# Six fewer transfers in a matmul with bias and residual: merged loads, merged last stores, and the residual added last for 24 tiles

## Chip, cores, metric

The kernel runs on one core of a Trainium2 chip. The metric is the device time of one execution in microseconds (us). The engines have short names: PE multiplies matrices (TensorE; PEld are its weight loads), ACT is ScalarE, DVE is VectorE, POOL is GpSimd, and SP (SyncE) issues the transfers; PSUM is the memory that PE's results land in, SBUF the one that holds the tiles. The granted clock is the share of PE's full clock that the throttle allowed.

## Reference

```python
batch, m, k, n = 16, 512, 1024, 768          # all float32
out = np.matmul(x, weight) + bias + residual # x: 16x512x1024, residual and out: 16x512x768
```

8192 rows are worked in 64 tiles of 128 rows. Eight tiles make a super tile: 128 partitions hold 8 neighbouring rows each, so a whole super tile of x is one transfer of 4 MB (32 KB in one piece per partition), and one of the residual or the output is 3 MB (24 KB per partition).

## The kernel before

x is cast to bf16 on ACT, transposed on PE, copied from PSUM to SBUF on DVE (`xt`), and multiplied on PE. There are two buffers for x, four for residual and output (`ro`, used in place), four for `tmp`. All loads and stores are issued in program order by SP.

```python
X_BUFS = 2; RO_BUFS = 4; TMP_BUFS = 4; EARLY = 12
def load_x(S, j0=0, j1=J):        # rows j0..j1 of super tile S, in one transfer
    ...
    K_(nc.sync.dma_start(out=x_sb[S][:, j0:j1, :], in_=x_d[S, :, j0:j1, :]))
# load_res and store are written the same way

def pool_add(t):                  # POOL: ro += tmp (early tiles), or ro += bias
    r = row(t)
    K_(nc.gpsimd.tensor_add(out=r, in0=r, in1=tmp[t] if t < EARLY else bias_sb))
def finish(t, n0=0, nl=N):        # DVE: empties PSUM
    p = po[t][:, n0:n0 + nl]
    if t < EARLY: tmp[t] = ring(...); nc.vector.tensor_add(out=tmp[t], in0=p, in1=bias_sb)
    else:         nc.vector.tensor_add(out=row(t, n0, nl), in0=p, in1=row(t, n0, nl))
# [...] start-up: x of super tile 0 in five pieces, the weights in four, residual 0 in two
    load_x(1, 0, 4)
    load_res(0, 4, 8)
    load_x(1, 4, 6)
    load_res(1, 0, 4)
    load_x(1, 6, 8)
    load_res(1, 4, 8)
# [...]
    for t in range(HEAD, n_t):
        cast(t + 2)
        S, j = divmod(t, J)
        if (t + 2) % J == J - 1:
            if S == 0:
                for j0 in (0, J // 2):
                    load_x(X_BUFS, j0, j0 + J // 2)
                    load_res(X_BUFS, j0, j0 + J // 2)
            else:
                load_x(S + X_BUFS)
                load_res(S + X_BUFS)
            if 1 <= S < n_s - 1:
                store(S - 1)
        # [...] the tile's 16 matmuls, with the transposes of tile t + 1 among them; finish; pool_add
        if S == n_s - 1 and j == 0:
            store(S - 1)
        if S == n_s - 1 and j == J // 2:
            store(S, 0, J // 2)
        if S == n_s - 1 and j > J // 2:
            store(S, j - 1, j)
    # [...] the last tile, in two column chunks, each finished and stored by itself
```

In the early tiles the sum of PSUM and bias goes to `tmp`, and POOL adds it to the residual when that has landed: DVE can empty PSUM without the residual. In the later tiles POOL adds the bias to the residual beforehand, and DVE needs both.

## Time and profile before

| | before |
|---|---|
| time, median of 6 runs | 211.26 us (211.13 to 211.57) |
| span of the profiled run | 209.4 us |
| PE busy | 200.6 us |
| share of the main DMA queue | 97.8% |
| moved by DMA | 87.2 MB |

The page of the profile, before: the busy line (busy us, share of the span, instructions), two lines of the slices (a digit is the share in a fortieth of the span, 9 for 90% or more), the DMA queues (packets, MB, share of 16 engines), and the chain that ended last.

```profile
...
PE 200.6 (96%) x1274; PEld 130.6 (62%) x1299; DVE 105.0 (50%) x139; ACT 67.6 (32%) x68; POOL 115.4 (55%) x71
...
DMA  6999999999999999999999999999999999999994
...
DMA packets 6208, 87.23 MB, mean 417 GB/s; under 512 B 689, under 2 KB 817, under 8 KB 2098
...
q1 hardware_dynamic: 6192, 87.03, 97.8%
q8 instruction: 10, 0.16, 0.3%
...
PE 95%; issue 1%; DVE 1%
PE po L104 79%; PE pt L95 13%; PE po L172 3%; PE po L192 1%; DVE xt L99 0%; DVE ro L131 0%; DVE warm L158 0%
...
```

PE and DMA are both full from start to end. The chain names PE for 95% of the span. PE ends at 203.2 us, the span is 209.4 us.

The end in stretches of 1 us, before: busy us of each engine with its count of instructions, then granted clock, mean busy share of the 16 DMA engines, GB/s. A share can come out a little over 1, since packets overlap by some ns.

```profile
...
core 0: us, PE busy (x) PEld busy (x) DVE busy (x) ACT busy (x) POOL busy (x), PEclk, DMA share, GB/s
...
201.00:202.00 1.00, 1.00 (x7) 0.42 (x5) 0.68 (x1) 0.00 (x0) 0.00 (x0) 1.00 0.98 409
202.00:203.00 1.00, 1.00 (x10) 0.75 (x8) 0.55 (x1) 0.00 (x0) 0.00 (x0) 1.00 0.99 406
203.00:204.00 1.00, 0.22 (x2) 0.00 (x0) 0.57 (x2) 0.00 (x0) 0.00 (x0) 1.00 0.95 384
204.00:205.00 1.00, 0.00 (x0) 0.00 (x0) 0.00 (x0) 0.00 (x0) 0.00 (x0) 1.00 1.03 404
205.00:206.00 1.00, 0.00 (x0) 0.00 (x0) 0.00 (x0) 0.00 (x0) 0.00 (x0) 1.00 0.73 283
206.00:207.00 1.00, 0.00 (x0) 0.00 (x0) 0.00 (x0) 0.00 (x0) 0.00 (x0) 1.00 0.41 151
207.00:208.00 1.00, 0.00 (x0) 0.00 (x0) 0.00 (x0) 0.00 (x0) 0.00 (x0) 0.76 0.11 39
...
```

PE stops at 203.2, DVE at 203.7. DMA works on at full share to 205 and then fades.

The casts of ACT that wait for x, before (start, us, what, and in brackets the idle time and what ended it). The casts at 51.34 are tiles 16 to 19, the first half of the third x.

```profile
...
36.60 2.00 ACT L87 CAST xb<-x_tile 128x1024 bf16<-128x1024 f32 x2 [2.30 <-DMA x_tile<-in_x_dram]
...
51.34 3.89 ACT L87 CAST xb<-x_tile 128x1024 bf16<-128x1024 f32 x4 [6.60 <-DMA x_tile<-in_x_dram]
59.93 2.00 ACT L87 CAST xb<-x_tile 128x1024 bf16<-128x1024 f32 x2 [4.70 <-DMA x_tile<-in_x_dram]
...
```

PE at the same place, before; the transposes of 128x128 at 55.99 us are tile 16's, one tile (3.04 us) after tile 15's.

```profile
...
52.96 0.60 PE L95 MATMUL pt<-ident,xb 128*128 128x128 f32 x4
...
55.99 0.60 PE L95 MATMUL pt<-ident,xb 128*128 128x128 f32 x4
...
```

### The profile page before, as it was taken

What the parts mean: (1) busy time and instruction counts of PE and PEld (TensorE: products, weight loads), DVE (VectorE), ACT (ScalarE), POOL (GpSimd) and SP (SyncE); (2) the same over time, 40 slices, a digit from 0 to 9 for tenths busy, and PEclk for the clock granted to TensorE, in tenths of its full rate; (3) what the DMA queues carried; (4) which work ended last, traced back from release to release, by engine and by line L of the source; (5) the groups of instructions that cost most, each with busy time, mean ns of one, the idle gap of its engine ahead of it and who ended that gap; (6) DMA issues with size and microseconds to landing.
All of it is one profiled execution on the core that took longest, in us unless ns stands there. A gap on an engine that the chain in (4) does not pass through costs nothing.

```text
span 209.4 us, 3156 instructions
## 1 busy us (share of the span) xinstructions
PE 200.6 (96%) x1274; PEld 130.6 (62%) x1299; DVE 105.0 (50%) x139; ACT 67.6 (32%) x68; POOL 115.4 (55%) x71
## 2 busy tenths in 40 slices
PE   7999999999999999999999999999999999999980
PEld 2556666666666666666666666666666666666640
DVE  0737465455445544554554455445445544555550
ACT  2544315331533062323433053230723133340000
POOL 2000197979999505991099702994069910799000
PEclk9999999999999999999999999999999999999998
DMA  6999999999999999999999999999999999999994
GB/s 237 427 425 427 429 416 428 418 441 419 432 457 440 408 423 426 444 419 435 432 429 435 427 419 446 437 426 423 418 435 437 457 405 416 441 433 430 408 404 155
DMA packets 6208, 87.23 MB, mean 417 GB/s; under 512 B 689, under 2 KB 817, under 8 KB 2098
## 3 DMA queue, kind: packets, MB, share of 16 engines
q1 hardware_dynamic: 6192, 87.03, 97.8%
q8 instruction: 10, 0.16, 0.3%
q14 instruction: 4, 0.03, 0.0%
q10 hardware_dynamic: 2, 0.00, 0.0%
HBM read 61.87 MB, written 25.17 MB: 416 GB/s over the span
## 4 chain that ended last, share of the span: by engine, by line
PE 95%; issue 1%; DVE 1%
PE po L104 79%; PE pt L95 13%; PE po L172 3%; PE po L192 1%; DVE xt L99 0%; DVE ro L131 0%; DVE warm L158 0%
## 5 line engine op out<-in xcount | busy, mean ns | idle before, releaser
L104 PE MATMUL po<-w_sb,xt 128*128 128x512 bf16 (+1 forms) x999 | 175.4, 324 | 1.4
L104 PEld LDWEIGHTS <-xt 128*128 128x128 bf16 x1024 | 100.1, 98 | 59.5 <-DVE xt L99 0.5
L121 POOL TENSOR_TENSOR ro<-ro,bias_sb 128x768 f32<-128x768 f32 x52 | 92.6, 1821 | 51.2 <-DMA ro<-in_residual_dram 41.3
L87 ACT CAST xb<-x_tile 128x1024 bf16<-128x1024 f32 x62 | 62.8, 1045 | 114.6 <-DMA x_tile<-in_x_dram 57.4
L99 DVE COPY xt<-pt 128x512 f32<-128x512 f32 x64 | 44.2, 692 | 86.8 <-PE pt L95 86.6
L131 DVE TENSOR_TENSOR ro<-po,ro 128x768 f32<-128x768 f32 (+2 forms) x53 | 49.4, 934 | 2.9 <-PE po L104 2.8
L95 PE MATMUL pt<-ident,xb 128*128 128x128 f32 x256 | 38.3, 273 | 0.0
L121 POOL TENSOR_TENSOR ro<-ro,tmp 128x768 f32<-128x768 f32 x12 | 21.5, 1817 | 26.2 <-DMA ro<-in_residual_dram 25.0
L95 PEld LDWEIGHTS pt<-ident,xb 128*128 128x128 f32 x256 | 29.8, 141 | 8.3 <-issue 0.8
L129 DVE TENSOR_TENSOR tmp<-po,bias_sb 128x768 f32<-128x768 f32 x12 | 11.4, 949 | 0.5 <-POOL ro L121 0.4
L172 PE MATMUL po<-warm 128*128 128x512 bf16 x15 | 6.0, 574 | 1.2 <-DVE warm L158 1.2
L178 ACT CAST w_sb<-ro 128x768 bf16<-128x768 f32 x4 | 3.3, 832 | 4.1 <-DMA ro<-in_weight_dram 4.1
L172 PEld LDWEIGHTS <-warm 128*128 128x128 bf16 x15 | 1.9, 135 | 4.1 <-issue 2.8
L87 DVE CAST xb<-x_tile 128x1024 bf16<-128x1024 f32 x2 | 1.4, 694 | 5.0 <-DMA x_tile<-in_x_dram 5.0
L180 DVE CAST w_sb<-ro 128x768 bf16<-128x768 f32 x4 | 2.2, 555 | 2.5 <-DMA ro<-in_weight_dram 2.5
L163 ACT ACT_TABLE_LOAD x1 | 1.3, 1283 | 2.0 <-POOL ident masks.py:199 2.0
L192 PE MATMUL po<-tmp 128*128 128x512 f32 (+1 forms) x4 | 1.5, 486 | 0.0
L200 DVE COPY bias_sb<-po 128x768 f32<-128x768 f32 x1 | 1.0, 958 | 0.1
L192 PEld LDWEIGHTS po<-tmp 128*128 128x128 f32 x4 | 0.7, 190 | 0.5 <-issue 0.5
L135 POOL MEMSET tmp<- 128x768 f32 x1 | 0.7, 737 | 0.3 <-POOLq L269 0.3
L158 DVE MEMSET warm<- 128x256 uint32 x1 | 0.3, 272 | 0.9 <-PEq L269 0.9
masks.py:199 POOL TENSOR_SCALAR_AFFINE_SELECT ident<-ident 128x128 f32<-128x128 f32 x1 | 0.3, 292 | 0.1
(8 smaller groups left out, 1.0 us busy)
## 6 DMA issues: line engine op xcount, KB each, us to landing
out_dram<-ro SPq DMA_DIRECT2D x7, 3072.0 KB, 24.2
x_tile<-in_x_dram SPq DMA_DIRECT2D x5, 4096.0 KB, 30.8
ro<-in_residual_dram SPq DMA_DIRECT2D x5, 3072.0 KB, 17.7
ro<-in_residual_dram SPq DMA_DIRECT2D x6, 1536.0 KB, 27.0
x_tile<-in_x_dram SPq DMA_DIRECT2D x3, 2048.0 KB, 25.6
x_tile<-in_x_dram SPq DMA_DIRECT2D x5, 1024.0 KB, 18.3
ro<-in_weight_dram SPq DMA_DIRECT2D x4, 768.0 KB, 9.1
out_dram<-ro SPq DMA_DIRECT2D x1, 1536.0 KB, 11.8
```

The costliest lines, as they stand in the source:

```text
L87: K_(copy(out=xb[t], in_=x_sb[t // J][:, t % J, :]))
L95: K_(nc.tensor.transpose(out=pt[:, c, :], in_=pairs[:, c * P:(c + 1) * P], identity=ident))
L99: K_(nc.vector.tensor_copy(out=xt[t], in_=pt))
L104: K_(nc.tensor.matmul(po[t][:, n0:n0 + nl], lhsT=both[:, e, :], rhs=w_sb[:, c, e, n0:n0 + nl], start=(i == 0), stop=(i == len(steps) - 1),))
L121: K_(nc.gpsimd.tensor_add(out=r, in0=r, in1=tmp[t] if t < EARLY else bias_sb))
L129: K_(nc.vector.tensor_add(out=tmp[t], in0=p, in1=bias_sb))
L131: K_(nc.vector.tensor_add(out=row(t, n0, nl), in0=p, in1=row(t, n0, nl)))
L163: K_(nc.scalar.copy(out=warm_a, in_=warm_a))
L172: K_(nc.tensor.matmul(warm_ps[:, 0:512], lhsT=warm[:, 0:P], rhs=warm, start=True, stop=True))
L178: K_(nc.scalar.copy(out=w_sb[:, c, e, :], in_=w_st[:, c, e, :]))
L180: K_(nc.vector.tensor_copy(out=w_sb[:, c, e, :], in_=w_st[:, c, e, :]))
L192: K_(nc.tensor.matmul(bias_ps[:, n0:n0 + nl], lhsT=ones, rhs=bias_row[:, n0:n0 + nl], start=True, stop=True,))
```

## The change

The intent: fewer and larger transfers, and the residual added last for tiles 12 to 23 too, because the residuals of these tiles now land later.

```diff
-EARLY = 12
+EARLY = 24
@@ start-up
-    load_x(1, 4, 6)
-    load_res(1, 0, 4)
-    load_x(1, 6, 8)
-    load_res(1, 4, 8)
+    load_x(1, 4, 8)
+    load_res(1)
@@ loop
-            if S == 0:
-                for j0 in (0, J // 2):
-                    load_x(X_BUFS, j0, j0 + J // 2)
-                    load_res(X_BUFS, j0, j0 + J // 2)
-            else:
-                load_x(S + X_BUFS)
-                load_res(S + X_BUFS)
+            load_x(S + X_BUFS)
+            load_res(S + X_BUFS)
@@ last stores
-        if S == n_s - 1 and j > J // 2:
-            store(S, j - 1, j)
+        if S == n_s - 1 and j == J - 1:
+            store(S, J // 2, j)
```

## The prediction

> **What bounds the kernel now.** Two things at once. The busy table has PE at 200.6 of 209.4 us, and the chain of waits is 95% PE without a gap above 0.05 us from 21 to 203 us: one tile costs 3.04 us (2.60 of matmuls, 0.44 of transposes). The queue table has the main DMA queue at 97.8%, the slices about 427 GB/s from 5 to 204 us. A super tile (8 tiles) moves 10.5 MB: 24.5 us at 427 GB/s, against 24.3 us of PE work. The Trainium skill ("DMA: Bandwidth & Descriptors", "Anatomy of one DMA") gives about 2 us of fixed cost per DMA; here transfers land 5 to 42 us after their issue because they queue, and the DMA share is about 1.0 in every stretch, so removing five of them frees next to nothing.
>
> **What the change does.**
> - Second x: rows 4-5 land with rows 6-7, about 2.5 us later (estimate: 1.05 MB at 427 GB/s; 36.6 becomes 39). Tile 12 is transposed at 43.85, so PE does not see it.
> - Third x as one 4 MB transfer. Before, its first half landed at 51.34 us (ACT's casts wait for it) and tile 16 was transposed at 55.99, 3.6 us of slack after the 1.05 us cast. The second half landed at 59.93 with 1.57 MB of residual between. Whole, it should land at 59.93 - 1.57/0.427 = 56.25 us. Cast until 57.3: PE should stop about 1.4 us before tile 16. That is on the critical path and PE does not win it back. This is the main cost.
> - Residual added last for tiles 12-23: DVE's add costs 949 against 934 ns, POOL's 1817 against 1821: free. It is needed: the second residual now lands whole near 46.4 us, the third near 63.6; the four tmp buffers let PSUM be emptied anyway (tile 12's add at 51.2 needs POOL's tile 8, done near 48.2). Neither should stop PE.
> - Last stores: rows 4-6 go as one 1.18 MB store when row 6 is finished (201.7 before). Before, row 4 went at about 195.6, DMA stayed busy to about 206, and the last store, issued at 204.0, landed 4.6 us later, behind a backlog. After, the queue runs dry (bytes before these stores end near 202.3), and 1.57 MB, 3.7 us, go out from about 204.7 (with PE 1.4 us late).
>
> **Sum.** +1.4 us PE stall, up to 0.8 us of it absorbed by the backlog at the end, +0.3 us for the emptied queue: about +0.9 us, 212.3 us. Range 211.2 to 213.6. Chances: faster by over 2% 0.01, within 2% 0.95, slower 0.04.
>
> **What would show it.** The chain of waits has a gap of 1 to 2 us near 56 us: PE waits for ACT's cast, the cast for the third x. PE's last matmul ends near 204.6 instead of 203.2; PE busy stays about 200.6. The DMA share falls under 0.8 for 1 to 2 us between 202 and 205. DMA at about 427 GB/s in the middle, no faster.
>
> **What would make it wrong.** Larger packets raising the DMA rate early (the third x lands before 55 us, nothing stalls: about 211.5); the merged load waiting longer at its slowest DMA engine (a stall of 2 to 3 us); tmp buffers holding back DVE, and with it PE, if the second residual lands after 49 us.

## The result

| | before | after |
|---|---|---|
| time, median of 6 runs | 211.26 us | 210.95 us (210.84 to 211.02) |
| ratio, 95% interval | | 0.9983 (0.997 to 0.9996) |
| span of the profiled run | 209.4 us | 209.1 us |
| PE's last matmul ends | 203.2 us | 204.4 us |

A ratio here is the mean time of one kernel's fast runs over the mean of the other's of the same rounds, so not quite the ratio of the medians. The change is worth 0.3 us, 0.17%; predicted were 0.9 us more. A repetition in another set of rounds, with 5 runs, gave 0.9983 again (below).

The page after:

```profile
...
PE 201.1 (96%) x1274; PEld 130.8 (63%) x1299; DVE 105.0 (50%) x139; ACT 68.0 (33%) x68; POOL 115.6 (55%) x71
...
DMA  6999999999999999999999999999999999999966
...
DMA packets 5344, 87.23 MB, mean 417 GB/s; under 512 B 593, under 2 KB 721, under 8 KB 1618
...
q1 hardware_dynamic: 5328, 87.03, 97.8%
...
PE 70%; DMA 25%; issue 1%; ACT 1%; DVE 0%; POOL 0%; ACTq 0%; POOLq 0%
PE po L104 60%; DMA x_tile<-in_x_dram 23%; PE pt L95 10%; DMA tmp<-in_bias_dram 2%; ACT xb L87 1%; DVE ro L131 0%; POOL ident masks.py:197 0%; ACTq L87 0%; POOL tmp L135 0%; POOLq L262 0%
...
```

The casts and PE near the third x, after:

```profile
...
38.95 3.93 ACT L87 CAST xb<-x_tile 128x1024 bf16<-128x1024 f32 x4 [4.70 <-DMA x_tile<-in_x_dram]
56.05 5.93 ACT L87 CAST xb<-x_tile 128x1024 bf16<-128x1024 f32 x6 [13.18 <-DMA x_tile<-in_x_dram]
...
```

```profile
...
53.29 0.60 PE L95 MATMUL pt<-ident,xb 128*128 128x128 f32 x4
...
57.15 0.66 PE L95 MATMUL pt<-ident,xb 128*128 128x128 f32 x4 [0.67 <-ACT xb L87]
...
```

The stop came as predicted. The third x landed whole at 56.05 us (56.25 was said), and tile 16 was transposed at 57.15 instead of 55.99, 1.16 us later. PE's idle time there is shorter, 57.15 - 53.29 - 3.04 = 0.82 us, because PE came to it 0.33 us later than before (tile 15 at 53.29 against 52.96). That difference comes from the start-up and wanders between runs: tile 15's start lies between 52.96 and 53.32 us in the twelve profiles looked at. It does not add to the delay, because x sets the time of tile 16: in the five profiles with the third x whole, ACT's casts of it start at 56.05 to 56.45 us, PE stops for 0.82 to 1.33 us (0.37 of it for DVE in one of them), and tile 16 follows at 57.15 to 57.55; in the others it is at 55.99 to 56.36. From tile 16 to PE's end it is 147.2 us before and 147.3 after. PE ended at 204.4 us, 1.2 us later than before. The chain changed as well: 23% of it is now a wait for x. Yet the kernel became faster. The end in stretches, after (columns as before):

```profile
...
201.00:202.00 1.00, 1.00 (x8) 0.60 (x7) 0.32 (x2) 0.00 (x0) 0.00 (x0) 1.00 0.67 283
202.00:203.00 1.00, 1.00 (x7) 0.43 (x5) 0.90 (x1) 0.00 (x0) 0.00 (x0) 1.00 0.32 135
203.00:204.00 1.00, 1.00 (x9) 0.71 (x8) 0.33 (x1) 0.00 (x0) 0.00 (x0) 1.00 0.41 172
204.00:205.00 1.00, 0.43 (x4) 0.14 (x2) 0.78 (x2) 0.00 (x0) 0.00 (x0) 1.00 1.05 442
205.00:206.00 1.00, 0.00 (x0) 0.00 (x0) 0.00 (x0) 0.00 (x0) 0.00 (x0) 1.00 1.01 406
206.00:207.00 1.00, 0.00 (x0) 0.00 (x0) 0.00 (x0) 0.00 (x0) 0.00 (x0) 1.00 0.85 340
207.00:208.00 1.00, 0.00 (x0) 0.00 (x0) 0.00 (x0) 0.00 (x0) 0.00 (x0) 1.00 0.68 238
...
```

From 201 to 204 us the DMA engines run dry, to a share of 0.32, because rows 4 to 6 are held until row 6 is finished. Then all of them work at full share to 206, and at 207 to 208 still 0.68 of them work, that is 11 engines, where before it was 1.8. Before, a few engines far behind the others ended the kernel; after, all end together.

### The profile page after: what moved, and what is told of

Its sections match the earlier page's. It is cut to its first block, busy times and chain, and to the rows that moved or that the text cites. A ratio compares the mean times of both kernels' runs of the same rounds, so it can differ in the third digit from the quotient of the medians.

```text
span 209.1 us, 3149 instructions
## 1 busy us (share of the span) xinstructions
PE 201.1 (96%) x1274; PEld 130.8 (63%) x1299; DVE 105.0 (50%) x139; ACT 68.0 (33%) x68; POOL 115.6 (55%) x71
## 4 chain that ended last, share of the span: by engine, by line
PE 70%; DMA 25%; issue 1%; ACT 1%; DVE 0%; POOL 0%; ACTq 0%; POOLq 0%
PE po L104 60%; DMA x_tile<-in_x_dram 23%; PE pt L95 10%; DMA tmp<-in_bias_dram 2%; ACT xb L87 1%; DVE ro L131 0%; POOL ident masks.py:197 0%; ACTq L87 0%; POOL tmp L135 0%; POOLq L262 0%
## 5 line engine op out<-in xcount | busy, mean ns | idle before, releaser
L121 POOL TENSOR_TENSOR ro<-ro,bias_sb 128x768 f32<-128x768 f32 x40 | 71.2, 1816 | 34.6 <-DMA ro<-in_residual_dram 24.6
L121 POOL TENSOR_TENSOR ro<-ro,tmp 128x768 f32<-128x768 f32 x24 | 43.1, 1816 | 42.3 <-DMA ro<-in_residual_dram 25.0
L131 DVE TENSOR_TENSOR ro<-po,ro 128x768 f32<-128x768 f32 (+2 forms) x41 | 38.0, 930 | 2.9 <-PE po L104 2.8
L129 DVE TENSOR_TENSOR tmp<-po,bias_sb 128x768 f32<-128x768 f32 x24 | 22.8, 949 | 0.4 <-PE po L104 0.4
```

The source lines that it names most:

```text
L129: K_(nc.vector.tensor_add(out=tmp[t], in0=p, in1=bias_sb))
L131: K_(nc.vector.tensor_add(out=row(t, n0, nl), in0=p, in1=row(t, n0, nl)))
```

## The experiments

**Theory A.** The DMA engine that is furthest behind sets the end of the kernel before. PE has slack, because the last stores queue behind that engine's backlog. The gain comes from the packets of the merged loads.
**Rival B.** The merge of the last stores gained, by fewer completions at the end, and the merged loads cost what PE stops.
**Rival C.** PE's end (or that of the stores) sets the time.

The trace lists every DMA packet with its start, duration and size. The tables below that give time by packet size, or follow one of the 16 engines, were worked out from these records: on one engine, a packet starts 3 or 4 ns before the one ahead of it ends, and every engine has the same sequence of sizes. Where packets of two engines ended at the same moment, the thread could be lost.

### One part alone: only the stores, only the loads

Only the stores:

```diff
 # from the kernel before
-        if S == n_s - 1 and j > J // 2:
-            store(S, j - 1, j)
+        if S == n_s - 1 and j == J - 1:
+            store(S, J // 2, j)
```

> The kernel before, with the last stores merged and nothing else. Theory A (the end is set by the DMA engine that is furthest behind; PE has slack): the merge saves only 0.06 us of packet time (24 packets of 3072 B at 121 ns become 8 of 9216 B at 356 ns on each engine), so the time is within 0.15 us of before. Rival B (the merged store is what gained, by two fewer completions at the end): at least 0.3 us faster than before. My prediction on record would say +0.2 to +0.3 us for an emptied queue.

Measured: 211.34 us against 211.64 for before in the same rounds, ratio 0.9986 (0.9967 to 1.0004). The interval holds both no gain and 0.3 us, so the time alone does not decide between A and B.

Only the loads (and `EARLY = 24`): the kernel after, with the lines above reversed.

> The kernel after, with the last stores row by row as before. PE still stops about 1.2 us near 56 us. Theory A (slowest DMA engine sets the end, larger packets made it faster): 0.2 to 0.4 us faster than before, like the kernel after. Rival B (stores gained, loads cost the PE stop): 0.8 to 1.2 us slower than before.

Measured: 211.53 us, ratio 0.9997 (0.9977 to 1.0017). PE stopped for 0.97 us near 56 us and ended at 204.6 us, and the time was not longer than before's: the 0.8 us that rival B wanted is outside the interval. The 0.2 us that theory A wanted cannot be told from nothing in these rounds (this chip's runs of before spread from 211.32 to 212.54).

What the times could not tell, the bytes can. MB moved by the main queue until 150 us, summed from the packet records of each profiled run:

```
loads as before                  loads merged
before          63.015           after           63.094
stores_only     62.981           loads_only      63.083
before_pe6      62.997           x2_split        63.063
before_pe20     62.979           after_pe6       63.075
                                 after_early12   63.092
                                 after_again     63.087
                                 x2_split_rows   63.079
```

The two groups do not overlap. The means are 62.993 and 63.082 MB; the difference of 0.089 MB is 0.21 us at 427 GB/s. It arises between 30 us (0.003 MB) and 65 us (0.121 MB), where the merged transfers flow, and stays at 0.09 to 0.12 MB. The run with `EARLY = 12` and merged loads is in the right-hand group, so `EARLY` is not the reason. (The failed run with the loads as before stands at 62.962; the run with quarter packets has other packets all through and is left out.) So the merged loads do make DMA faster, by 0.2 us. The packet sizes are the likely reason, since they are what the merge changes there: the median packet of 8 KB took 311 ns (38.9 ns per KB), of 16 KB 614 ns (38.4), of 32 KB 1213 ns (37.9). The sum agrees: all packets of the main queue, less 3.5 ns of overlap each, take 203.50 to 203.76 us per engine in the four runs on the left and 203.31 to 203.41 in the seven on the right. That the gain in time at the end is this 0.2 us is not shown by this run, whose time shows no gain; the last run below (x2_split_rows) is the better test.

### PE without its stop: the third x in two halves

```diff
 # from the kernel after
-            load_x(S + X_BUFS)
+            if S == 0:
+                load_x(X_BUFS, 0, J // 2)
+                load_x(X_BUFS, J // 2, J)
+            else:
+                load_x(S + X_BUFS)
             load_res(S + X_BUFS)
```

> The kernel after, with the third x as two halves one after the other (no residual between), so that PE does not stop near 56 us: the first half should land near 51.3 us, and PE should end near 203.2 us instead of 204.4. Theory A: the time is that of the kernel after, plus at most 0.15 us for packets of 16 KB instead of 32 KB. Rival C (PE's end sets the time): 0.8 to 1.2 us faster than the kernel after, that is 1.1 to 1.5 us faster than before.

ACT, then PE, of this run near tile 16:

```profile
...
51.37 3.89 ACT L87 CAST xb<-x_tile 128x1024 bf16<-128x1024 f32 x4 [8.32 <-DMA x_tile<-in_x_dram]
...
```

```profile
...
53.03 0.60 PE L95 MATMUL pt<-ident,xb 128*128 128x128 f32 x4
...
56.07 0.60 PE L95 MATMUL pt<-ident,xb 128*128 128x128 f32 x4
...
```

The first half landed at 51.4 us, PE went through tile 16 without a stop (56.07 = 53.03 + 3.04) and ended at 203.3 us, as expected. The time: 211.29 us, ratio to before 0.9975 (0.9957 to 0.9993), against 0.9983 for the kernel after. Rival C asked for 1.1 to 1.5 us over before, that is 0.995 or less, which the interval excludes. The end in stretches shows where PE's 1.1 us went:

```profile
...
201.00:202.00 1.00, 1.00 (x6) 0.45 (x5) 0.76 (x1) 0.00 (x0) 0.00 (x0) 1.00 0.66 283
202.00:203.00 1.00, 1.00 (x9) 0.78 (x8) 0.48 (x1) 0.00 (x0) 0.00 (x0) 1.00 0.68 283
...
207.00:208.00 1.00, 0.00 (x0) 0.00 (x0) 0.00 (x0) 0.00 (x0) 0.00 (x0) 0.50 0.10 40
...
```

From 201 to 203 us part of the engines ran dry (0.66, 0.68), because the stores still waited for row 6. At 207 to 208 the share was 0.10 again: 1.6 engines worked on alone, and they ended the kernel whatever PE did. The last packet ended at 208.6 us.

### PE made slower, in both kernels

```diff
 def mms(t, i):
     if i == 0:
         po[t] = psum_o(t)
+        if t == 30:      # n = 6 or 20 matmuls that the tile's own first one overwrites
+            both = xt[t][:, 0, :].bitcast(BF16).rearrange("p (m e) -> p e m", e=2)
+            for _ in range(n):
+                K_(nc.tensor.matmul(po[t][:, 0:512], lhsT=both[:, 0, :],
+                                    rhs=w_sb[:, 0, 0, 0:512], start=True, stop=True))
```

> The kernel before, with six more matmuls of 512 columns (216 ns each, 1.3 us of PE) ahead of tile 30, into PSUM that the tile's own first matmul overwrites; the result is right. Theory A: PE has about 3 us of slack at the end (row 7's stores are issued at 203.2 us and the slowest DMA engine reaches them only near 207), so within 0.15 us of before. Rival C (PE is the bound): 1.3 us slower.

> The kernel after, with the same six matmuls (1.3 us of PE) ahead of tile 30. Theory A: the merged store of rows 4 to 6 began at 203.76 us, just when the slowest DMA engine became free (203.83 us), so no slack is left: 1.0 to 1.3 us slower than the kernel after, 0.7 to 1.1 us slower than before. If the kernel after still had slack, it would stay at 0.3 us faster than before.

> The kernel before, with twenty more matmuls (4.3 us of PE) ahead of tile 30. Theory A: about 3 us of it vanish in the backlog at the end, so 0.9 to 1.8 us slower than before. Rival C (PE is the bound): 4.3 us slower. If DMA alone counted with no limit: same as before.

| added to | PE time added | measured | ratio to before | longer than before |
|---|---|---|---|---|
| before, 6 matmuls | 1.29 us | 211.62 us | 0.9997 (0.998 to 1.0014) | 0.0 us |
| after, 6 matmuls | 1.29 us | 212.49 us | 1.0051 (1.0039 to 1.0064) | 1.1 us (the kernel after: -0.3) |
| before, 20 matmuls | 4.32 us | 212.91 us | 1.0071 (1.0059 to 1.0084) | 1.5 us |

The last column is the difference of the medians of the same rounds; the kernel after was not in these rounds, its -0.3 is from others. Against before, all three are as theory A said (against the kernel after, 1.4 us where 1.0 to 1.3 was said). The kernel before gives away 1.3 us of PE time for nothing. Of 4.3 us it feels 1.5, so its slack on the PE side is about 2.8 us. The kernel after, given the same 1.3 us, loses all of it: its own later PE, and stores that wait for row 6, had used its slack up. The stretches of 2 us of both runs with six matmuls, before first:

```profile
...
201.00:203.00 2.00, 2.00 (x12) 1.08 (x11) 1.32 (x2) 0.00 (x0) 0.00 (x0) 1.00 0.97 404
203.00:205.00 2.00, 1.56 (x12) 0.88 (x9) 1.12 (x3) 0.00 (x0) 0.00 (x0) 1.00 0.85 340
...
```

```profile
...
201.00:203.00 2.00, 2.00 (x16) 1.40 (x14) 1.13 (x2) 0.00 (x0) 0.00 (x0) 1.00 0.45 190
203.00:205.00 2.00, 2.00 (x12) 0.93 (x11) 0.96 (x1) 0.00 (x0) 0.00 (x0) 1.00 0.07 31
205.00:207.00 2.00, 1.01 (x9) 0.66 (x7) 1.12 (x2) 0.00 (x0) 0.00 (x0) 1.00 0.89 369
...
```

Before with six more matmuls has no gap like that: 0.97, 0.85. After with six more stands at 0.07 from 203 to 205 us, 1.1 engines: nearly all are dry, so that the stores' start alone sets the end.

### The move of the residual add

```diff
 # from the kernel after
-EARLY = 24
+EARLY = 12
```

> The kernel after with the bias (and not the residual) added by POOL from tile 12 on, as before. The second residual lands whole near 46.4 us, so POOL's add for tile 12 ends near 53.6 us where DVE wants it at 51.2, and for tile 16 near 65.4 where DVE wants it at 64.5. Theory A: PE stops up to 2 us in total beyond its 1.2 us, and the merged last store leaves no slack: 0.3 to 2 us slower than the kernel after. If the move of the residual add is of no use: same as the kernel after.

Measured: 211.45 us, ratio to before 1.0004 (0.9991 to 1.0016); the kernel after had 0.9983 in two other sets of rounds, so the gain seems gone (compared across rounds, and the intervals touch). PE near tile 16 of this run:

```profile
...
55.53 1.48 PE L104 MATMUL po<-w_sb,xt 128*128 128x512 bf16 x8 [0.37 <-DVE xt L99]
57.55 0.66 PE L95 MATMUL pt<-ident,xb 128*128 128x128 f32 x4 [0.55 <-ACT xb L87]
...
```

Without the move PE did wait for DVE, 0.37 us at 55.5 us; the kernel after has no such wait. But it came just before the stop for x, which became shorter by it (0.55 us): x was cast from 56.45 us on here, and tile 16 followed at 57.55. From there to PE's end (204.8 us) it is 147.3 us, as in the kernel after. So this profile shows no loss of PE from leaving the move out, and what became of the gain stays open.

### Packets a quarter of the size

```diff
 # from the kernel before, for the fourth to the eighth super tile
-                load_x(S + X_BUFS)
-                load_res(S + X_BUFS)
+                for j0 in range(0, J, 2):
+                    load_x(S + X_BUFS, j0, j0 + 2)
+                for j0 in range(0, J, 2):
+                    load_res(S + X_BUFS, j0, j0 + 2)
```

> The kernel before, with x and residual of the fourth to the eighth super tile each in four transfers of two rows, in the same order. PE's data arrives no later. Theory A: packets of 8 KB at 311 ns instead of 32 KB at 1213 ns for x, 6 KB at 234 ns instead of 24 KB at 912 ns for the residual, and 30 more completions add about 2.0 to 2.4 us to each DMA engine's packet time (estimate from the packet times of before), and the time grows by the same, 2 us. Rival C (PE is the bound): within 0.2 us of before.

Measured: 213.53 us, ratio 1.0099 (1.0084 to 1.0115), 2.1 us longer, as theory A said. Its page:

```profile
...
PE 200.3 (95%) x1274; PEld 130.6 (62%) x1299; DVE 105.0 (50%) x139; ACT 68.6 (32%) x68; POOL 115.4 (54%) x71
...
DMA packets 10529, 87.24 MB, mean 412 GB/s; under 512 B 1169, under 2 KB 1297, under 8 KB 5138
...
```

PE's busy time is what it was (200.3), and PE's last matmul ended at the same 203.2 us as before. Only DMA has more to do: 10,529 packets for the same bytes instead of 6,208. What a transfer costs beside its bytes does count here, although every transfer is queued behind others. The edit makes 30 more transfers as well as smaller packets; each transfer has one 4-byte packet of 9 ns on every engine, so at most 0.27 of the 2.1 us goes to the number of transfers, as far as the packet records show it.

### More instruction fetches (failed)

Which engines are the late ones? Here the engines are followed through the packet records of the run described next, whose last stores go row by row and so do not hold the engines up together. All 16 can be followed from the sequence of sizes that each of them runs through; where two ended a packet at the same moment, their fetches can be exchanged.

```
x2_split_rows: the end of each engine, us, and the instruction fetches on it
205.38 to 205.55   six engines     none (four), or one of 8 KB (two; 0.31 us each)
206.14 to 206.26   four engines    one of 16 KB each (0.98 to 1.10 us)
206.42 to 206.47   three engines   one of 16 KB (two), or two of 8 KB
207.07             one engine      none, or one of 16 KB (the thread is not sure)
208.08 and 208.12  two engines     two of 16 KB each (2.0 and 2.1 us together)
```

There are ten packets of 16 KB in the queue that the profile calls "instruction", one every 18 to 21 us. In the kernel before, the two engines that ended last (207.73 and 207.97 us) had two of them each, and so had the last two in the runs with only the stores, with only the loads, and with the third x in halves. The records also show how the lag arises. In the kernel before, a fetch of 16 KB takes 0.94 to 1.10 us of its engine, the kernel's next packet there takes 0.37 to 0.50 us more than the median of its size, so the engine falls back by 1.3 to 1.6 us and stays there: the one with the first fetch (22.0 us) was 1.5 us behind the median of the engines without a fetch at 25 us, and still at 172. After their second fetches the last two were 2.9 and 2.7 us behind, about the slack of 2.8 us found above. One engine fell 1.8 us behind without a fetch. So the records tie the lag to the fetches; no run has changed the fetches alone. The attempt to prove it:

```diff
 # from the kernel before, in the loop
+        if t >= 24:
+            for _ in range(24):
+                K_(nc.gpsimd.memset(tiny, 0.0))   # two elements; nothing waits for it
```

> The kernel before with 24 memsets of two elements on POOL (about 35 ns each) in every tile from 24 on, where POOL has room; nothing waits for them. They only make POOL's program longer by 960 instructions, which have to be fetched by the same DMA engines. In the packet records the two engines that end last in before carried two 16 KB instruction fetches each (about 1.05 us each), the others one or none. Theory D (fetches make the engine that ends last): about 60 KB more is fetched, the engines with most fetch time end last again, and the time grows by 0.2 to 1.5 us, according to which engines get them. Rival: the lag has another cause, and the time stays within 0.15 us of before.

Measured: 291.14 us, ratio 1.376, at a granted clock of 0.90. The experiment failed: one such memset in a row starts 147 ns after the one before it (24 in 3.47 us) and not 35, so POOL became the bound, and DVE waited for it.

```profile
...
POOL 57%; DMA 26%; issue 15%; SPq 1%; ACT 0%; POOLq 0%; ACTq 0%
...
L245 POOL MEMSET tiny<- 1x2 f32 x960 | 85.5, 89 | 53.1
...
L131 DVE TENSOR_TENSOR ro<-po,ro 128x768 f32<-128x768 f32 (+2 forms) x53 | 49.7, 939 | 127.1 <-POOL tiny L245 127.1
...
```

The additional fetches came, seven more of 8 KB, but DMA no longer set the end: the run says nothing about what fetches cost. (35 ns was the step between four memsets at the start of the program, which overlap.)

### The kernel after again, and the version with the most slack

> The kernel after, unchanged, on the chip of the other two: theory A says 0.1 to 0.4 us faster than before (the merged loads put the DMA engines about 0.09 MB, 0.2 us, ahead by 100 us in every run with merged loads so far).

Measured: 211.19 us against 211.54, ratio 0.9983 (0.9969 to 0.9997). The small gain of the change is repeated.

```diff
 # from the kernel after: the third x in two halves as above, and
-        if S == n_s - 1 and j == J - 1:
-            store(S, J // 2, j)
+        if S == n_s - 1 and j > J // 2:
+            store(S, j - 1, j)
```

> The kernel after with the third x in two halves and the last stores row by row: PE neither stops at 56 us nor do stores wait for row 6. This has the most slack on the PE side. Theory A: the engine that ends last sets the time alone, so it is no better than the kernel after, within 0.25 us, and 0.1 to 0.4 us faster than before. Rival C (PE or the stores set the time): at least 0.6 us faster than the kernel after.

Measured: 211.19 us, ratio 0.9981 (0.9966 to 0.9996), the same as the kernel after on the same chip. Neither an early PE nor early stores buy anything: rival C falls again. This run also answers rival B: it has merged loads (all but the third x, which is in halves), `EARLY = 24` and the stores of before, and it gained 0.35 us, with an interval that excludes 1. So the merged stores are not needed for the gain. None of the versions clearly beats the kernel after.

## Why the prediction was wrong

The range was 211.2 to 213.6 us, and the time was 210.95. The direction was wrong: I forecast 0.9 us more, and it became 0.3 us less. Term by term:

| term of the sum | predicted | measured |
|---|---|---|
| PE's stop before tile 16 | +1.4 us | tile 16 1.16 us later (PE idle 0.82 us; 0.82 to 1.33 in five profiles) |
| of it absorbed at the end | up to 0.8 us | all (1.29 us of PE added to the kernel before: 0.0 us longer) |
| queue emptied by the merged stores | +0.3 us | not seen (only the stores: 0.7 us faster to 0.1 us slower); the engine that is furthest behind did not run dry |
| five transfers fewer | next to nothing | -0.2 us (from the bytes moved until 150 us) |

- **Right:** the third x landing whole at 56.25 us (56.05), the cast and PE's stop there, PE's last matmul near 204.6 us (204.4), unchanged PE work, and the dip of the DMA share near the end (0.67 to 0.32 for 3 us; under 0.8 for 1 to 2 us was said). Not shown: that the residual move is needed.
- **The step that failed:** "That is on the critical path and PE does not win it back." It is on PE's chain, but PE's chain did not end the kernel. The kernel before can lose 1.3 us of PE without any effect and has about 2.8 us of slack (PE made slower). I saw the backlog and let it absorb at most 0.8 us, because I measured it with the mean of the 16 engines: "bytes before these stores end near 202.3". But a transfer has landed when its last engine is done. By the packet records, the engines of the kernel after finished those bytes between 200.8 and 203.8 us. The merged store was issued at 202.93 and its first packets began at 203.75 (I had said 204.7), just as the last engine became free. For fourteen engines the queue ran dry, for the last it did not, and only that one counts. The Trainium skill ("DMA: Bandwidth & Descriptors", "Why a DMA increments its semaphore by 16 and not by 1") says that up to 16 engines share a transfer, finish independently and are counted by the semaphore; this trace agrees: 688 packets of 4 bytes for 43 transfers before, 592 for 37 after, 16 each, and the 16 engines ended between 205.1 and 208.0 us before.
- **The term set to nothing:** "removing five of them frees next to nothing". The waits of single transfers are hidden by the queue, but the sizes of their packets are not. Merged loads moved DMA ahead by 0.2 us in all seven profiles that have them. On a kernel whose DMA engines set the end, this is the whole of the expected gain. I had named the case as one that would make me wrong ("larger packets raising the DMA rate early") and tied it to a landing before 55 us; it came without that.
- **Two effects met by chance.** Later PE and held-back stores (a loss that was absorbed) and larger packets (a small gain) belong to the same change. It used up the slack, as far as these rounds can tell: six more matmuls cost the kernel before nothing and the kernel after 1.4 us against its own time (ratios 1.0051 and 0.9983).

What stays open: what the end would be without the instruction fetches (in the records the late engines fall behind at them; the test failed), why one engine fell behind without one, whether merging the stores has an effect of its own (its interval reaches from 0.7 us faster to 0.1 us slower), and why the run with `EARLY = 12` showed no gain.

## What to carry to other kernels

When PE and DMA are both full, ask which of them ends the kernel, and look for it in the last microseconds: a DMA share that fades through 0.4 and 0.1 says that a few engines are behind, and they set the end. A stop on the other engine then costs nothing until the slack is used up; measure that slack by adding work, because the chain of waits does not show it. And when DMA sets the end, count packets and their sizes rather than transfers, by the engine that is last and not by the mean.

## What the Trainium skill lacked or had wrong

- "DMA: Bandwidth & Descriptors" gives the cost of a transfer issued from GpSimd as about 2 us plus bytes over the rate ("Anatomy of one DMA"), and a rule of 1 MiB or more ("Rules for kernel authors"). Nothing in it says what packets of 8 to 32 KB cost in a queue that is always full, with transfers of 1 MB and more in both cases: here 38.9 ns per KB in packets of 8 KB, 38.4 in 16 KB, 37.9 in 32 KB, and 2.1 us of 211 for a quarter of the packet size in most loads.
- The same page says that the engines finish independently, but not by how much they drift apart in a kernel that is DMA-bound throughout: 2.9 us (205.1 to 208.0 us) among the 16 engines before.
- "Runtime: NRT & Kernel Launch" ("Instruction fetch mechanics") has the program fetched in blocks of 16 KiB and calls the cost mostly hidden. The trace agrees with the size (ten packets of 16,384 bytes in 209 us), but each occupied one of the 16 DMA engines for 0.94 to 1.10 us and set it back by 1.3 to 1.6 us with the longer packet after it, and the engines that carried two were the last to end. No page says what a fetch costs the kernel's own transfers; no run here changed the fetches alone.
- No page gives the time of many small POOL instructions in a row: 147 ns from one memset of two elements to the next (89 ns busy).
